# Attention and merge of a hybrid S5, attention and MoE layer: the work of GpSimd handed to VectorE and ScalarE, and VectorE operations joined in pairs

## The chip, the cores and the metric

The kernel runs on one core of one Trainium2 chip. The metric is the device time of one execution in microseconds (us); lower is better. All data are fp32. A matrix product is made from three products of split operands (high by high, high by low, low by high), so each operand exists as a high part and a low part.

## The reference, cut to what matters

One layer on 1024 latent tokens of width 1024, with 256 context tokens. The change touches the middle of it:

```python
p = softmax(concat([s_loc, s_ctx, sink], axis=-1))       # 8 heads; band of 3 blocks of 128 keys, 256 context keys
o = p_loc @ v_band + p_ctx @ v_ctx
z = gelu(y_ssm);  z = z * sigmoid(z @ w_glu + b_glu)
m = sigmoid(g_ssm) * (z @ w_ssm_out) + sigmoid(g_att) * (o @ w_att_out)
h = layer_norm(alpha * h + gate1 * (m @ w_o))
```

After it come the router, the mixture of experts (MoE, 32 experts, four for each token) and a last layer norm.

## The kernel before, in words

**Order of the work.** `pre` (line 143) holds everything ahead of the experts: input projections, the S5 scan, attention, GLU and merge; `moe` and `finish` follow. The stage of the change begins near 570 us and ends where the ranking of tokens by expert begins, near 1115 us. Attention (line 513) is the main stream there. `Filler.emit` (line 127) puts pieces of a second stream between its parts, 5.0 us of stated cost at a time (`FILL`), and the second stream is `tail` (line 217): `glu`, `ssm_out`, then `merge`. With every piece of `glu` and `ssm_out` goes one step of `residual` (line 708). Outside of `manual_schedule` blocks the framework's planner settles each engine's order when the kernel is built, from the written order and its own costs; inside such a block the engines that it names keep the written order. The end of `merge` (after `K.last`) keeps VectorE's written order. Each engine runs its instructions in the order that was settled, and all transfers of this stage are issued from one queue, SP.

**Attention.** Eight blocks of 128 queries, two groups of four heads. A call of `scores` (line 566) treats a pair of heads: matmuls to two `sa` tiles (128x384, local keys) and one `sb` tile (128x512, context keys of both heads) in PSUM; VectorE's maxima (lines 589, 590); then on 128x2 tiles the steps of lines 591 to 594 that give minus the maximum (`nm`) and the sink's exponent; ScalarE's exponentials into `P` with their sums (lines 598 to 603); VectorE's total and reciprocal (lines 604 to 606). At line 608 GpSimd (POOL) multiplies the two `P` tiles by it. There are 32 pairs, so 64 such products, 48 of 640 columns and 16 of 512. `values` (line 611) transposes `P` on TensorE, splits the transposes into `ph` (ScalarE) and `pl` (VectorE, line 43) and multiplies them with V.

**GLU.** `glu` (line 465) takes 256 tokens at a time, four times: per block `m` of 128 channels 12 matmuls into 256 columns of a PSUM bank of its own, a sigmoid on ScalarE (line 488), a product (line 489), a split into `K.zh` and `K.zl`. The PSUM pool `mm` has two banks.

**Merge.** `merge` (line 754) has four groups of 256 tokens; group g starts when attention has finished its two blocks of 128 queries. `branches` (line 806): 12 matmuls with `w_att_out` per block of 128 columns, a product with the gate (line 823), a sum (line 824), a split into `mh` and `ml` (line 825). `mix` (line 833), for groups 0 to 2: 24 matmuls per 128 tokens and 256 columns with `w_o`, a product (line 842) and a sum (line 843) into `h`. `norm` (line 850) makes layer norm and modulation, whose last sum (line 862) is POOL's. Group 3 goes through `mix_tile`, one tile of 128 tokens at a time.

**Weights of the merge.** `weights` (line 793) keeps up to two pieces of 1 MiB ready: it loads a piece raw and splits it, the high part on ScalarE, the low part in turn on POOL and VectorE (`eng=`, line 795). Over the four groups that are 22 pieces, eleven of them on POOL; two more pieces of `w_o` are split at line 242, so 24 in all. The same six pieces return for each group. Tiles `raw`, `whi` and `wlo` have two buffers each.

**Other work on POOL.** `residual` (lines 716, 721, 722) scales `xhat_d` by ALPHA and the gains, 16 pieces of 128x512 through memory and back; `consts` (lines 776 to 780); `residual2` (line 1552) makes two products of 128x512 for each tile of tokens, from memory for tiles 0 to 5 (`h is None`), from the tile on hand for 6 and 7.

Of the kernel before, what the change touches and what calls it, by code (L numbers as in the profile page):

```python
# [8 lines left out]
F32 = mybir.dt.float32  # L9
# [10 lines left out]
D = 1024  # L20
# [61 lines left out]
def body(tc, a, o):  # L82
# [3 lines left out]
    with es:  # L86
# [21 lines left out]
        K.cst = cst  # L108
        K.mask = cst.tile([128, 8, 2, 32], BF16, name="mask")
# [33 lines left out]
def pre(tc, a, K, top):  # L143
    nc = tc.nc
    es = ExitStack()
    with es:
# [88 lines left out]
        with ExitStack() as ws:  # L235
# [6 lines left out]
            K.wo = [load_w(tc, K, a["w_o"][:, c * 256:(c + 1) * 256], to=[wo.tile([128, KT, 256], F32R, name="wo%d%d" % (c, i)) for i in range(2)])  # L242
                    for c in range(2)]
# [221 lines left out]
def glu(tc, a, K, zp):  # L465
# [3 lines left out]
    for c in range(4):  # L469
# [13 lines left out]
        for m in range(4):  # L483
            p = K.mm.tile([128, 512], F32, tag="mm", name="mm")
            p = p[:, 0:256]
            mm3(nc, p, w, (zh, zl), 4, lambda x, k: x[:, k, m * 128:(m + 1) * 128], lambda x, k: x[:, k, :])
            g = zp.tile([128, 256], F32, tag="zsig", bufs=2, name="zsig")
            nc.scalar.activation(out=g, in_=p, func=ACTF.Sigmoid, bias=K.cols[:, 48 + m:49 + m])
            nc.vector.tensor_tensor(g, g, zt[:, m, :], ALU.mult)
            split(nc, K.zh[:, m, t0:t0 + 256], K.zl[:, m, t0:t0 + 256], g)  # L490
            if m % 2:
                yield 2.8
# [20 lines left out]
def attention(tc, a, K, es, fl):  # L513
# [16 lines left out]
    nc.sync.dma_start(out=sink, in_=a["sink"].unsqueeze(0).to_broadcast([128, 8]))  # L530
    KH = kp.tile([128, 2, S + NCTX], F32R, name="KH")
# [34 lines left out]
    def scores(n, kv, pr, Q):  # L566
# [25 lines left out]
        nc.vector.scalar_tensor_tensor(nm, nm, 0.125, sink[:, hs], ALU.mult, ALU.max)  # L592
        nc.vector.tensor_tensor(su[:, 2], sink[:, hs], nm, ALU.subtract)
        nc.vector.tensor_scalar(nm, nm, -1.0, None, ALU.mult)
# [9 lines left out]
        nc.vector.tensor_tensor(su[:, 0], su[:, 0], su[:, 1], ALU.add)  # L604
        nc.vector.tensor_tensor(su[:, 0], su[:, 0], su[:, 2], ALU.add)
        nc.vector.reciprocal(su[:, 0], su[:, 0])  # L606
        for i in range(2):
            nc.gpsimd.tensor_scalar(P[i][:, 0:nl + 256], P[i][:, 0:nl + 256], su[:, 0, i:i + 1], 1.0, ALU.mult, ALU.mult)  # L608
# [99 lines left out]
def residual(tc, a, K, es):  # L708
# [3 lines left out]
    for c in range(2):  # L712
# [3 lines left out]
        nc.gpsimd.tensor_scalar(gb, gb, ALPHA, 1.0, ALU.mult, ALU.mult)  # L716
        for t in range(8):
# [3 lines left out]
            nc.gpsimd.tensor_tensor(x, x, gb[:, 0], ALU.mult)  # L721
            nc.gpsimd.tensor_tensor(x, x, gb[:, 1], ALU.add)
# [30 lines left out]

def merge(tc, a, K, es):
# [16 lines left out]
    def consts():  # L771
# [4 lines left out]
        nc.gpsimd.tensor_tensor(x0, x0, G2, ALU.mult)  # L776
        nc.gpsimd.tensor_tensor(B2, B2, x0, ALU.add)
        x0 = hp.tile([128, D], F32, tag="xm", name="x0")
        nc.sync.dma_start(out=x0, in_=a["ln_rows"][0:1, :].to_broadcast([128, D]))
        nc.gpsimd.tensor_tensor(G2, G2, x0, ALU.mult)  # L780
# [7 lines left out]
    sources = [s for g in range(4) for s in  # L788
               [(a["w_att_out"][:, c * 512:(c + 1) * 512], 512, 4) for c in range(2)] +
               [(a["w_o"][:, c * 256:(c + 1) * 256], 256, 8) for c in range(0 if g < 3 else 2, 4)]]  # L790
    ready = []

    def weights():
        while len(ready) < 2 and sources:
            ready.append(load_w(tc, K, *sources.pop(0), eng=nc.gpsimd if len(sources) % 2 else None))
        return ready.pop(0)
# [9 lines left out]
    def branches(g, raw, gs, mh, ml):  # L806
# [5 lines left out]
        for c in range(4):  # L812
# [179 lines left out]
    for g in range(4):  # L992
# [25 lines left out]
        for t in late:  # L1018
            yield t
# [1225 lines left out]
```

## Time and profile before

| | |
|---|---|
| median of 3 runs | 2791.53 us (2789.71 to 2792.7) |
| the profiled execution | 2796.39 us, span 2794.6 us |
| busy over the span | TensorE (PE) 90%, VectorE (DVE) 80%, ScalarE (ACT) 52%, GpSimd (POOL) 17% |
| TensorE's granted clock, mean | 0.943 of 2.4 GHz |
| moved by DMA | 631.11 MB, mean 226 GB/s |

The span is cut into 40 slices on the profile's page, so the stage of the change is slices 9 to 16. A busy engine is not an engine at its peak. Idle time in a row is charged to what ended it. DMA share is the mean busy share of the 16 DMA engines.

### The profile page before, as it was taken

To read this page: it belongs to the slowest core of one execution; us is meant where nothing else is said; L and a number is where in the kernel's file an instruction comes from. 1 tells how busy PE (TensorE), PEld (TensorE's weight loads), DVE (VectorE), ACT (ScalarE), POOL (GpSimd) and SP (SyncE) were. 2 spreads that over 40 slices of the span, in tenths; PEclk is the share of its full clock that TensorE was granted. 3 is DMA by queue.
4 is the path that set the end of the run, shared out by engine and by line. 5 is a ranking of instruction groups with operands and counts; after the bars stand their busy time and mean duration, and the time that the engine had idled before them with its cause. 6 is when DMAs were issued, how large, how long until landed. Compare 5 with 4: busy or idle time off the path is not lost. (4 is left out here: it accounts for less than half of the span.)

```text
span 2794.6 us, 41588 instructions
## 1 busy us (share of the span) xinstructions
PE 2523.9 (90%) x14030; PEld 2123.3 (76%) x14030; DVE 2234.2 (80%) x4306; ACT 1465.9 (52%) x2352; POOL 465.0 (17%) x303
## 2 busy tenths in 40 slices
PE   6799999978887877699999999999999999999990
PEld 1698887767686767588888888889888887888770
DVE  9636796347788887788878888888988899899995
ACT  0623113656555422455656666666666666666661
POOL 3200000034333243210110110110111011101113
PEclk8799999979998877699999999999999999999995
DMA  7434623554454463678979978988998999899983
GB/s 252 155 125 157 202 87 116 161 172 136 163 169 139 146 195 102 209 244 266 290 226 284 295 242 283 292 273 272 303 294 262 305 301 300 275 305 302 311 280 144
DMA packets 409674, 631.11 MB, mean 226 GB/s; under 512 B 36497, under 2 KB 215569, under 8 KB 408497
## 3 DMA queue, kind: packets, MB, share of 16 engines
q1 hardware_dynamic: 397152, 584.37, 63.8%
q0 software_dynamic: 11872, 42.47, 6.5%
q8 instruction: 112, 1.84, 0.3%
q10 hardware_dynamic: 432, 1.57, 0.2%
q14 instruction: 106, 0.86, 0.1%
HBM read 551.76 MB, written 76.57 MB: 225 GB/s over the span
## 5 line engine op out<-in xcount | busy, mean ns | idle before, releaser
L1478 DVE TENSOR_TENSOR wl<-raw,wh 128x1024 fp32r<-128x1024 f32 x768 | 920.8, 1219 | 163.4 <-ACT wh L1476 162.3
L1476 ACT ACTIVATE wh<-raw 128x1024 fp32r<-128x1024 f32 x768 | 790.3, 1052 | 246.5 <-PE dn L1294 87.9
L1344 PE MATMUL uw<-x,wh 128*128 128x320 f32 (+5 forms) x1920 | 581.3, 366 | 0.2 <-issue 0.2
L1345 PE MATMUL uw<-x,wl 128*128 128x192 f32 (+4 forms) x1920 | 501.4, 261 | 0.0
L1344 PEld LDWEIGHTS uw<-x,wh 128*128 128x128 f32 x1920 | 364.3, 190 | 24.0 <-issue 0.3
L1345 PEld LDWEIGHTS uw<-x,wl 128*128 128x128 f32 x1920 | 369.6, 193 | 0.5
L1291 PE MATMUL dn<-wh,a 128*128 128x512 f32 (+4 forms) x752 | 298.7, 397 | 0.0
L1292 PE MATMUL dn<-wl,a 128*128 128x512 f32 (+4 forms) x752 | 293.6, 390 | 0.0
L1427 POOL DMA_INDIRECT acc_d<-y,wi x47 | 120.4, 2562 | 958.3 <-DVE y L1425 816.3
L1294 PE MATMUL dn<-wh,a 128*128 128x512 f32 (+3 forms) x608 | 238.5, 392 | 0.6 <-DVE a L1271 0.6
L1291 PE MATMUL up<-wh,x 128*128 128x512 f32 x544 | 221.8, 408 | 0.0
L1294 PE MATMUL up<-wh,x 128*128 128x512 f32 x544 | 213.0, 392 | 0.0
L1292 PE MATMUL up<-wl,x 128*128 128x512 f32 x544 | 212.3, 390 | 0.0
L1356 ACT ACTIVATE t<-uw,bias 128x160 f32<-128x160 f32 (+5 forms) x240 | 98.6, 419 | 134.5 <-PE uw L1345 131.6
L1291 PEld LDWEIGHTS dn<-wh,a 128*128 128x128 f32 (+4 forms) x752 | 135.7, 180 | 37.8 <-issue 4.1
L1292 PEld LDWEIGHTS dn<-wl,a 128*128 128x128 f32 (+4 forms) x752 | 135.8, 181 | 33.9
L608 POOL TENSOR_SCALAR P<-P,su 128x640 f32<-128x640 f32 (+1 forms) x64 | 55.1, 874 | 608.0 <-DVE su L606 543.9
L1294 PEld LDWEIGHTS dn<-wh,a 128*128 128x128 f32 (+3 forms) x608 | 112.8, 186 | 28.4 <-DVE a L1271 2.7
L42 ACT ACTIVATE whi<-raw 128x2048 fp32r<-128x2048 f32 x38 | 72.8, 1917 | 112.9 <-PE mm L53 72.5
L1240 POOL DMA_INDIRECT x<-xm_d,ri x47 | 53.3, 1135 | 463.3 <-DVE L L1202 304.0
L1291 PEld LDWEIGHTS up<-wh,x 128*128 128x128 f32 x544 | 102.3, 188 | 27.4 <-issue 8.4
L1294 PEld LDWEIGHTS up<-wh,x 128*128 128x128 f32 x544 | 102.1, 188 | 22.4
(532 smaller groups left out, 5349.2 us busy)
## 6 DMA issues: line engine op xcount, KB each, us to landing
raw<-w_gate_up SPq DMA_DIRECT2D x512, 512.0 KB
raw<-w_down SPq DMA_DIRECT2D x256, 512.0 KB
mw<-w_mod SPq DMA_DIRECT2D x64, 256.0 KB
raw<-w_o SPq DMA_DIRECT2D x16, 1024.0 KB
raw<-w_in SPq DMA_DIRECT2D x13, 1024.0 KB
raw<-w_mod SPq DMA_DIRECT2D x8, 1024.0 KB
gate_d<-gs SPq DMA_DIRECT2D x16, 512.0 KB
raw<-w_att_out SPq DMA_DIRECT2D x8, 1024.0 KB
```

Source lines behind the costliest of these rows:

```text
L42: nc.scalar.activation(out=hi, in_=src, func=ACTF.Copy)
L608: nc.gpsimd.tensor_scalar(P[i][:, 0:nl + 256], P[i][:, 0:nl + 256], su[:, 0, i:i + 1], 1.0, ALU.mult, ALU.mult)
L1240: nc.gpsimd.indirect_dma_start(out=x[0:nb], out_offset=None, in_=K.xm_d, bounds_check=S - 1, oob_is_err=True, in_offset=bass.IndirectOffse ...
L1291: nc.tensor.matmul(ps, lhsT=h, rhs=wh[:, k], start=st, stop=False)
L1292: nc.tensor.matmul(ps, lhsT=h, rhs=wl[:, k], start=False, stop=en and nb <= 64)
L1294: nc.tensor.matmul(ps, lhsT=X[:, k0 + k, lo:lo + nb], rhs=wh[:, k], start=False, stop=en)
L1344: nc.tensor.matmul(p[:, 0:2 * n], lhsT=wh[:, k, fs], rhs=self.x[:, k, 0:2 * n], start=k == 0, stop=False)
L1345: nc.tensor.matmul(p[:, 0:m], lhsT=wl[:, k, fs], rhs=self.x[:, k, 0:m], start=False, stop=k == KT - 1)
L1356: nc.scalar.activation(out=y[i], in_=self.uw[i][:, 1], func=ACTF.Identity, bias=self.bias[:, q * 8 + j0 + i:q * 8 + j0 + i + 1])
L1427: nc.gpsimd.indirect_dma_start(out=K.acc_d, out_offset=bass.IndirectOffsetOnAxis(ap=wi[0:nb], axis=0), in_=o[0:nb], in_offset=None, bounds ...
L1476: nc.scalar.activation(out=h, in_=r, func=ACTF.Copy)
L1478: nc.vector.tensor_tensor(l, r, h, ALU.subtract)
```

## The change: what it does

- GLU: two blocks of 128 channels share one PSUM bank, each with its own matmuls and sigmoid; product and split are made once on 512 columns.
- Softmax: the sign is taken into a constant (`nsink`), and the total is one `reduce_sum`; lines 591 to 594 and 604 to 606 become five operations. The products with `P` go to ScalarE.
- Residual, constants, the last sum of `norm`, and `residual2` for tiles 0 to 5 go from POOL to VectorE. Tiles 6 and 7 keep POOL.
- Weights: `parts` splits each of the six pieces once (ScalarE and VectorE), writes both parts to memory, and loads both parts (2 MiB) at every later use, 18 times.
- Merge: both blocks of a step share one PSUM bank; product, sum and split are made on 512 columns. `h` becomes one tile of 128x2x1024.

```diff
@@ -239,8 +241,7 @@
...
             residual2_consts(tc, a, K, pool(ws, "res2"))
-            K.wo = [load_w(tc, K, a["w_o"][:, c * 256:(c + 1) * 256], to=[wo.tile([128, KT, 256], F32R, name="wo%d%d" % (c, i)) for i in range(2)])
-                    for c in range(2)]
+            K.wo = [parts(tc, a, K, "o", c, [wo.tile([128, KT, 256], F32R, name="wo%d%d" % (c, i)) for i in range(2)]) for c in range(2)]
             while not K.last:
...
@@ -480,16 +481,17 @@
...
         yield 1.0
-        for m in range(4):
+        for m in (0, 2):
             p = K.mm.tile([128, 512], F32, tag="mm", name="mm")
-            p = p[:, 0:256]
-            mm3(nc, p, w, (zh, zl), 4, lambda x, k: x[:, k, m * 128:(m + 1) * 128], lambda x, k: x[:, k, :])
-            g = zp.tile([128, 256], F32, tag="zsig", bufs=2, name="zsig")
-            nc.scalar.activation(out=g, in_=p, func=ACTF.Sigmoid, bias=K.cols[:, 48 + m:49 + m])
-            nc.vector.tensor_tensor(g, g, zt[:, m, :], ALU.mult)
-            split(nc, K.zh[:, m, t0:t0 + 256], K.zl[:, m, t0:t0 + 256], g)
-            if m % 2:
-                yield 2.8
+            g = zp.tile([128, 2, 256], F32, tag="zsig", bufs=2, name="zsig")
+            for j in range(2):
+                n = m + j
+                pj = p[:, j * 256:(j + 1) * 256]
+                mm3(nc, pj, w, (zh, zl), 4, lambda x, k: x[:, k, n * 128:(n + 1) * 128], lambda x, k: x[:, k, :])
+                nc.scalar.activation(out=g[:, j], in_=pj, func=ACTF.Sigmoid, bias=K.cols[:, 48 + n:49 + n])
+            nc.vector.tensor_tensor(g, g, zt[:, m:m + 2, :], ALU.mult)
+            split(nc, K.zh[:, m:m + 2, t0:t0 + 256], K.zl[:, m:m + 2, t0:t0 + 256], g)
+            yield 2.8
 
...
@@ -528,6 +530,8 @@
...
     nc.sync.dma_start(out=sink, in_=a["sink"].unsqueeze(0).to_broadcast([128, 8]))
+    nsink = cp.tile([128, 8], F32, name="nsink")
+    nc.vector.tensor_scalar(nsink, sink, -1.0, None, ALU.mult)
     KH = kp.tile([128, 2, S + NCTX], F32R, name="KH")
...
@@ -589,9 +593,8 @@
...
         nc.vector.tensor_tensor(nm, mx[:, 0], mx[:, 1], ALU.max)
-        nc.vector.scalar_tensor_tensor(nm, nm, 0.125, sink[:, hs], ALU.mult, ALU.max)
-        nc.vector.tensor_tensor(su[:, 2], sink[:, hs], nm, ALU.subtract)
-        nc.vector.tensor_scalar(nm, nm, -1.0, None, ALU.mult)
+        nc.vector.scalar_tensor_tensor(nm, nm, -0.125, nsink[:, hs], ALU.mult, ALU.min)
+        nc.vector.tensor_tensor(su[:, 2], sink[:, hs], nm, ALU.add)
         P = []
...
@@ -601,11 +604,10 @@
...
         nc.scalar.activation(out=su[:, 2], in_=su[:, 2], func=ACTF.Exp)
-        nc.vector.tensor_tensor(su[:, 0], su[:, 0], su[:, 1], ALU.add)
-        nc.vector.tensor_tensor(su[:, 0], su[:, 0], su[:, 2], ALU.add)
-        nc.vector.reciprocal(su[:, 0], su[:, 0])
+        nc.vector.reduce_sum(nm, su.rearrange("p a i -> p i a"), axis=AX.X)
+        nc.vector.reciprocal(nm, nm)
         for i in range(2):
-            nc.gpsimd.tensor_scalar(P[i][:, 0:nl + 256], P[i][:, 0:nl + 256], su[:, 0, i:i + 1], 1.0, ALU.mult, ALU.mult)
+            nc.scalar.activation(out=P[i][:, 0:nl + 256], in_=P[i][:, 0:nl + 256], func=ACTF.Copy, scale=nm[:, i:i + 1])
         return P
...
@@ -713,13 +715,13 @@
...
         nc.sync.dma_start(out=gb, in_=a["ln_rows"][2:4, cs].unsqueeze(0).to_broadcast([128, 2, 512]))
-        nc.gpsimd.tensor_scalar(gb, gb, ALPHA, 1.0, ALU.mult, ALU.mult)
+        nc.vector.tensor_scalar(gb, gb, ALPHA, None, ALU.mult)
         for t in range(8):
...
             nc.sync.dma_start(out=x, in_=d)
-            nc.gpsimd.tensor_tensor(x, x, gb[:, 0], ALU.mult)
-            nc.gpsimd.tensor_tensor(x, x, gb[:, 1], ALU.add)
+            nc.vector.tensor_tensor(x, x, gb[:, 0], ALU.mult)
+            nc.vector.tensor_tensor(x, x, gb[:, 1], ALU.add)
             nc.sync.dma_start(out=d, in_=x)
...
@@ -751,6 +753,22 @@
...
 
+def parts(tc, a, K, m, c, to=None):
+
+    nc = tc.nc
+    kt, n = (4, 512) if m == "a" else (KT, 256)
+    hi, lo = to or (K.wp.tile([128, kt, n], F32R, tag=t, name=t) for t in ("whi", "wlo"))
+    if (m, c) in K.parts:
+        for t, d in zip((hi, lo), K.parts[m, c]):
+            nc.sync.dma_start(out=t.bitcast(F32), in_=d)
+    else:
+        load_w(tc, K, a["w_att_out" if m == "a" else "w_o"][:, c * n:(c + 1) * n], n, kt, to=(hi, lo))
+        K.parts[m, c] = [K.dram.tile([128, kt, n], F32, name="w%s%d%d" % (m, c, i)) for i in range(2)]
+        for t, d in zip((hi, lo), K.parts[m, c]):
+            nc.sync.dma_start(out=d, in_=t.bitcast(F32))
+    return hi, lo
+
+
 def merge(tc, a, K, es):
...
@@ -773,11 +791,11 @@
...
         nc.sync.dma_start(out=x0, in_=a["ln_rows"][1:2, :].to_broadcast([128, D]))
-        nc.gpsimd.tensor_tensor(x0, x0, G2, ALU.mult)
-        nc.gpsimd.tensor_tensor(B2, B2, x0, ALU.add)
+        v.tensor_tensor(x0, x0, G2, ALU.mult)
+        v.tensor_tensor(B2, B2, x0, ALU.add)
         x0 = hp.tile([128, D], F32, tag="xm", name="x0")
         nc.sync.dma_start(out=x0, in_=a["ln_rows"][0:1, :].to_broadcast([128, D]))
-        nc.gpsimd.tensor_tensor(G2, G2, x0, ALU.mult)
+        v.tensor_tensor(G2, G2, x0, ALU.mult)
         x0 = hp.tile([128, D], F32, tag="xm", name="x0")
...
@@ -785,14 +803,12 @@
...
 
-    sources = [s for g in range(4) for s in
-               [(a["w_att_out"][:, c * 512:(c + 1) * 512], 512, 4) for c in range(2)] +
-               [(a["w_o"][:, c * 256:(c + 1) * 256], 256, 8) for c in range(0 if g < 3 else 2, 4)]]
+    sources = [s for g in range(4) for s in [("a", c) for c in range(2)] + [("o", c) for c in range(0 if g < 3 else 2, 4)]]
     ready = []
...
         while len(ready) < 2 and sources:
-            ready.append(load_w(tc, K, *sources.pop(0), eng=nc.gpsimd if len(sources) % 2 else None))
+            ready.append(parts(tc, a, K, *sources.pop(0)))
         return ready.pop(0)
...
@@ -815,14 +831,13 @@
...
                 w = weights()
+            p = K.mm.tile([128, 512], F32, tag="mm", name="mm").rearrange("p (i n) -> p i n", i=2)
             for i in range(2):
                 n = c % 2 * 2 + i
-                p = K.mm.tile([128, 512], F32, tag="mm", name="mm")[:, 0:256]
-                mm3(nc, p, w, (oh, ol), 4, lambda x, k: x[:, k, n * 128:(n + 1) * 128], lambda x, k: x[:, k, :])
-                u = gt[:, i, :]
-                v.tensor_tensor(u, p, u, ALU.mult)
-                v.tensor_tensor(u, u, sm[:, i, :], ALU.add)
-                split(nc, mh[:, c * 2 + i, :], ml[:, c * 2 + i, :], u)
+                mm3(nc, p[:, i], w, (oh, ol), 4, lambda x, k: x[:, k, n * 128:(n + 1) * 128], lambda x, k: x[:, k, :])
+            v.tensor_tensor(gt, p, gt, ALU.mult)
+            v.tensor_tensor(gt, gt, sm, ALU.add)
+            split(nc, mh[:, c * 2:c * 2 + 2, :], ml[:, c * 2:c * 2 + 2, :], gt)
             yield 2.7
...
@@ -835,12 +850,11 @@
...
             rn = part(g, c + 1) if c < 3 else None
+            p = K.mm.tile([128, 512], F32, tag="mm", name="mm").rearrange("p (i n) -> p i n", i=2)
             for i in range(2):
-                p = K.mm.tile([128, 512], F32, tag="mm", name="mm")[:, 0:256]
-                mm3(nc, p, (mh, ml), w, KT, lambda x, k: x[:, k, i * 128:(i + 1) * 128], lambda x, k: x[:, k, :])
-                u = gp.tile([128, 256], F32, tag="u", bufs=1, name="u")
-                v.tensor_tensor(u, p, g1[:, cs], ALU.mult)
-                v.tensor_tensor(h[i][:, cs], u, r[:, i, :], ALU.add)
+                mm3(nc, p[:, i], (mh, ml), w, KT, lambda x, k: x[:, k, i * 128:(i + 1) * 128], lambda x, k: x[:, k, :])
+            v.tensor_tensor(h[:, :, cs], p, g1[:, cs].unsqueeze(1).to_broadcast([128, 2, 256]), ALU.mult)
+            v.tensor_tensor(h[:, :, cs], h[:, :, cs], r, ALU.add)
             r = rn
...
@@ -859,14 +873,14 @@
...
             v.tensor_tensor(x, h[i], G2, ALU.mult)
-            nc.gpsimd.tensor_tensor(x, x, B2, ALU.add)
+            v.tensor_tensor(x, x, B2, ALU.add)
             nc.sync.dma_start(out=K.xm_d[t * 128:(t + 1) * 128, :], in_=x)
...
         t = 6 + i
-        h = hp.tile([128, D], F32, tag="h", name="h")
+        h = h67[:, i]
         st = K.sm2.tile([128, 4, 6], F32, tag="l3st", name="l3st")
...
@@ -1013,8 +1027,9 @@
...
             break
-        h = [hp.tile([128, D], F32, tag="h", name="h") for _ in range(2)]
+        h = hp.tile([128, 2, D], F32, tag="h", bufs=1, name="h")
         yield from mix(g, r, mh, ml, h, late)
+        h = [h[:, i] for i in range(2)]
         for t in late:
...
@@ -1025,6 +1040,7 @@
...
 
+    h67 = hp.tile([128, 2, D], F32, tag="h", bufs=1, name="h")
     for h6, gates6, modulated6 in mix_tile(0, mh, ml, late):
...
@@ -1549,7 +1565,7 @@
...
             x = h[:, cs]
-        nc.gpsimd.tensor_tensor(x, x, K.ga[:, cs], ALU.mult)
+        (nc.gpsimd if h is not None else v).tensor_tensor(x, x, K.ga[:, cs], ALU.mult)
         xs.append(x)
...
     for c, x in enumerate(xs):
```

## Rows read from the trace of the kernel before

**Rows 1.** Windows: length; PE, PEld, DVE, ACT, POOL busy; PE clock, DMA share, GB/s.
```profile
570.00:665.00 95.00, 68.35 (x388) 58.68 (x388) 55.50 (x98) 57.49 (x114) 52.01 (x44) 0.80 0.47 158
665.00:750.00 85.00, 79.10 (x429) 63.13 (x428) 61.44 (x142) 48.15 (x122) 20.09 (x18) 1.00 0.43 145
750.00:955.00 205.00, 165.05 (x1138) 145.84 (x1136) 173.06 (x420) 106.59 (x269) 75.71 (x49) 0.90 0.47 152
955.00:1070.00 115.00, 82.78 (x491) 73.46 (x490) 89.47 (x164) 37.40 (x58) 45.77 (x23) 0.78 0.60 192
```

**Rows 2.** What TensorE waited for, 570 to 1070: total us, times, longest.
```profile
PE pv L633 <- DVE pl L43: 15.8, 7, 3.7
PE pv L632 <- DVE of L642: 11.9, 3, 7.0
PE tp L621 <- issue: 11.8, 1, 11.8
PE sa L583 <- ACT P L598: 10.7, 8, 3.9
PE mm L51 <- DVE gg L823: 10.3, 3, 5.6
PE tp L933 <- POOL xm L862: 8.0, 1, 8.0
...
PE mm L51 <- ACT zsig L488: 3.6, 3, 2.1
```

**Rows 3.** Timeline of VectorE: start us, duration us, instruction.
```profile
834.11 0.16 DVE L594 TENSOR_SCALAR nm<-nm 128x2 f32<-128x2 f32 x1
...
849.11 3.98 DVE L594 TENSOR_SCALAR nm<-nm 128x2 f32<-128x2 f32 x1
```

**Rows 4.** Timeline of GpSimd over the same time.
```profile
848.56 4.50 POOL L43 TENSOR_TENSOR wlo<-raw,whi 128x2048 fp32r<-128x2048 f32 x1
```

**Rows 5.** Windows 570 to 1070 by tile: su, nm, zsig, gg, u; DVE busy first.
```profile
570.00:1070.00 500.00, 35.16 (x124) 6.26 (x31) 53.78 (x62) 0.87 0.49 161
570.00:1070.00 500.00, 41.99 (x124) 65.65 (x248) 0.87 0.49 161
570.00:1070.00 500.00, 22.29 (x32) 13.79 (x32) 0.87 0.49 161
570.00:1070.00 500.00, 52.17 (x96) 12.70 (x32) 0.87 0.49 161
570.00:1070.00 500.00, 24.48 (x48) 0.87 0.49 161
```

**Rows 6.** Groups on VectorE, 570 to 1070: busy us, mean ns | idle before.
```profile
L43 DVE TENSOR_TENSOR wlo<-raw,whi 128x2048 fp32r<-128x2048 f32 x13 | 30.7, 2362 | 7.0 <-ACT whi L42 7.0
...
L593 DVE TENSOR_TENSOR su<-sink,nm 128x2 f32<-128x2 f32 x31 | 13.7, 442 | 0.8
...
L508 DVE TENSOR_TENSOR gs<-mm,gs 128x512 f32<-128x512 f32 x16 | 11.0, 688 | 3.4 <-PE mm L53 3.1
```

**Rows 7.** The page's costliest group (expert stage).
```profile
L1478 DVE TENSOR_TENSOR wl<-raw,wh 128x1024 fp32r<-128x1024 f32 x768 | 920.8, 1219 | 163.4 <-ACT wh L1476 162.3
```

**Rows 8.** Groups on GpSimd, 570 to 1130, with what ended its idle time.
```profile
L721 POOL TENSOR_TENSOR x<-x,gb 128x512 f32<-128x512 f32 x16 | 21.8, 1364 | 18.4 <-DMA x<-xhat_d 18.2
...
L1552 POOL TENSOR_TENSOR x<-x,ga 128x512 f32<-128x512 f32 x12 | 17.6, 1482 | 37.4 <-DMA x<-xhat_d 19.5 <-DVE pT L1116 15.3 <-DVE x L1561 2.6
```

**Rows 9.** Groups on ScalarE, 570 to 1070.
```profile
L42 ACT ACTIVATE whi<-raw 128x2048 fp32r<-128x2048 f32 x24 | 46.1, 1920 | 43.5 <-PE mm L53 23.3 <-PE mm L52 13.0 <-DVE h L843 7.2
...
L42 ACT ACTIVATE mh<-gg 128x256 fp32r<-128x256 f32 x32 | 12.7, 420 | 34.8 <-DVE gg L824 34.7
```

**Rows 10.** DMA from 570 to 1070, all queues.
```profile
DMA packets 58474, 80.54 MB, mean 161 GB/s; under 512 B 6792, under 2 KB 40712, under 8 KB 58248
```

**Rows 11.** SP's queue, a transfer of 1536 KB: start and duration of its issue.
```profile
745.75 0.47 SPq L772 DMA_DIRECT2D rb<-rows_d  x1
```

**Rows 12.** VectorE's first reader of that transfer.
```profile
755.71 0.69 DVE L773 TENSOR_SCALAR rb<-rb 128x1024 f32<-128x1024 f32 x1 [0.24 <-DMA rb<-rows_d]
```

More of the change, by code (lines that the diff above doesn't have):

```diff
@@ L108, in body @@
         K.cst = cst
+        K.dram = dram
+        K.parts = {}
         K.mask = cst.tile([128, 8, 2, 32], BF16, name="mask")
@@ L950, in choose @@
         su = K.sm2.tile([128, 1], F32, tag="tsu", name="tsu")
-        oh = gp.tile([128, 256], F32, tag="u", bufs=1, name="oh")[:, 0:128].rearrange("p (k e) -> p k e", k=4)
+        oh = gp.tile([128, 128], F32, tag="u", bufs=1, name="oh").rearrange("p (k e) -> p k e", k=4)
         over = oh.rearrange("p k e -> p e k")
```

## The prediction

> **What bounds the kernel now.** I read the windows of the stage first, then what TensorE waits for, then the timelines of VectorE and GpSimd at the worst gap, last the groups of each engine. In the 500 us from 570 to 1070 TensorE is busy for 68.35 + 79.10 + 165.05 + 82.78 = 395.3 us and idle for 104.7 us [rows 1]. Only the second stretch is close to TensorE's own rate (79.1 of 85 us, clock 1.00). In the others the clock is 0.80, 0.90 and 0.78, a mixture of 2.4 and 1.2 GHz; as time at the lower level that is 0.4 x 95 + 0.2 x 205 + 0.44 x 115 = 130 us, and it lies where TensorE has its gaps. So the stage is not bound by one engine's total; it is a chain that passes through TensorE, VectorE and ScalarE, and the names behind TensorE's gaps are mostly VectorE's [rows 2].
>
> Why VectorE is late is in the timelines. An operation on 128x2 elements takes 0.16 us at 834.11 and 3.98 us at 849.11 [rows 3]; the second began while GpSimd split a weight piece, a job of 4.50 us that began at 848.56, and ended as that ended [rows 4]. The same shows in sums. The seven small softmax operations cost 35.16 + 41.99 - 13.7 = 63.5 us for 31 pairs (line 593 stands in both tile rows) [rows 5, 6], 2.05 us a pair where seven bare ones would be 1.12. So GpSimd's 52.0 + 20.1 + 75.7 + 45.8 = 193.6 us [rows 1] cost little by themselves, but hold VectorE up.
>
> **The change part by part.** VectorE first, with a bare 512-wide product at 0.69 us [rows 6] and a 1024-wide one at 1.22 us [rows 7].
> - Softmax: 32 pairs x 2.05 = 65.6 us become 32 x 5 x 0.16 = 25.6 (the new sum over six columns is priced as a small operation; ends 0.16 and 0.69 would make it 17 us more at worst). Saves 40.
> - GLU: 22.3 us [rows 5] become 16 x 0.69 = 11.0. Saves 11.
> - Branches: 52.2 us [rows 5] become 16 x 3 x 0.69 = 33.1. Saves 19.
> - Mix: 24.5 us [rows 5] become 12 x 2 x 0.69 = 16.6. Saves 8.
> - Weights: thirteen of the splits at 2.36 us [rows 6] become six. Saves 16.5.
> - Moved in from GpSimd: 32 + 12 operations of 512 columns (residual, residual2) at 0.69 and 11 of 1024 (constants, norm) at 1.22. Adds 30.4 + 13.4 = 44.
> Net about -51 us of VectorE's 379 in the stage [rows 1], with no GpSimd to wait for.
>
> ScalarE gets 64 scalings of P. From 0.42 us for 256 columns and 1.92 for 2048 [rows 9] a column is 0.84 ns, so 0.74 us for 640 and 0.63 for 512: 48 x 0.74 + 16 x 0.63 = 46 us. GpSimd's own time, 53.8 us [rows 5], is the upper end, if the scale from a tile costs more. It loses 18 weight splits, 18 x 1.92 = 35 us, and some 5 us by wider copies. Net +6 us on 250 [rows 1]: hidden, since ScalarE is half idle; were it not, the whole 46 would stand behind the reciprocal of each pair.
>
> DMA: 24 loads of 1 MiB become 6 loads, 12 stores and 36 loads, 30 MiB or 31.5 MB more. The shares of rows 1 make 247 us of all 16 engines for 80.54 MB [rows 10], 326 GB/s; so the addition is 97 us, and the sum 344 us fits into a stage of some 450. SP issues 30 transfers more, 30 x 0.47 = 14 us [rows 11], and in its queue a load that waits for a weight buffer stands before those for gates, sums and queries. A load of parts can start only when the matmuls of the piece before the last have freed its buffer; it then has the time of one piece to land. A load of 1.5 MiB was issued at 745.75 and its reader ran at 755.71, 10 us later [rows 11, 12], so 2 MiB takes up to 13 us, and 6.4 us at the full rate. By the code a group uses six pieces; the third stretch covers a little over two groups, so some thirteen pieces in 205 us, 16 us each, and eight in the 115 us of the fourth, 14 us each. I take this at nothing; the cover is attention's work between two pieces, thin in the fourth stretch.
>
> GLU puts two blocks into one bank, with the sigmoid of the first between their matmuls. No row shows TensorE at a bank that ScalarE is reading. The nearest is TensorE's wait for the sigmoid to free a bank, 2.1 us at the longest [rows 2]: between 0 and 8 x 2.1 = 17 us. I take 4, as attention's matmuls can stand between. The Trainium skill, PSUM — Partial Sum Buffer, section on bank collisions, says that two engines may not touch one bank in the same partitions at a time and that software must keep them apart; by it the second half would always wait, and the sum would come out 13 us higher, near 2758.
>
> VectorE also takes over waits for transfers: GpSimd stood 18.2 us before line 721 and 19.5 us before line 1552 until data came [rows 8]. On GpSimd nothing queued behind; on VectorE the softmax does, and TensorE behind that. Ends 0 and 37.7 us; I take 2, the low side, since the planner orders VectorE by when data should be there. The products of line 1552 for the last two tiles stand in VectorE's written order, on the path: 4 x 0.69 = 3 us.
>
> **What it gives back.** Of TensorE's waits [rows 2] those that GpSimd makes go: 11.9 (line 642), 10.3 (823) and 8.0 (its own sum at 862). Half of the 11.8 goes (the first transposes, behind softmax steps held up in the same way), and a third of 15.8 (pl) and of 10.7 (exponentials, behind line 594); the rest of these is their normal chain, and becomes the next late thing. That is 11.9 + 10.3 + 8.0 + 5.9 + 5.3 + 3.6 = 45 us. With fewer gaps the clock is up for longer. The 130 us at the lower level cost at most half of TensorE's work in them, 0.5 x 0.79 x 130 = 51 us; I take a fifth, 10 us, since the gaps shrink rather than vanish. 45 + 10 - 4 - 2 - 3 = 46 us. The profiled execution took 2796.4 us (span 2794.6 and 1.8 around it), so 2750.4 by its time; it lies 4.9 us above the median of the runs, 2791.5, so the forecast is **2745 us**. The expert stage behind is untouched and moves forward as a whole.
>
> **Rivals.**
> - TensorE becomes the bound: all waits of rows 2 but the sigmoid's go (68.5 us) and half of the clock's cost (25 us), 2698 us. For it: VectorE falls to 328 us. Against: the chains of softmax and GLU stay serial.
> - The shared bank always holds TensorE: 17 us in place of 4, 2758 us. For it: the sigmoid stands between the matmuls in the written order. Against: there are other matmuls to run.
> - VectorE stands behind transfers: 37.7 us in place of 2, 2781 us. For it: rows 8, and more traffic. Against: the residual has a whole group's time.
> - **Slower: reloaded weights come late.** If pieces follow each other at their own matmuls' pace, 48 matmuls at 85 / 429 = 0.20 us [rows 1] are 9.5 us against 13.3 us of landing: 3.8 us each, 18 x 3.8 = 68 us against 46 gained, 2813 us. It decides from 12 late pieces on (46 / 3.8). For it: the depth of prefetch falls from raw and split pairs to split pairs alone, and the share is 0.60 in the last stretch. Against: 16 us between pieces while attention runs, which holds for most of them.
> - It moves nothing: the planned order hands the freed time to other waits, 2791 us.
>
> **How the numbers follow.** Chances: forecast 0.50, TensorE as the bound 0.13, bank 0.12, VectorE behind transfers 0.09, late weights 0.10, nothing 0.06. What a measurement of this kernel can tell from no change is about 0.2%, 5.6 us. Faster: 0.50 + 0.13 + 0.12 + 0.09 = 0.84; within it 0.06; slower 0.10. The range from 2700 to 2785 holds the forecast with its bounds, both milder rivals and nearly all of the first; outside are late weights and no change, and a little of the best case.
>
> **What would show it.** Right: GpSimd all but empty from 570 to 1060; small softmax operations at 0.16 us each, none above 1 us; VectorE near 330 us in the stage; TensorE's waits for lines 642, 823 and 862 gone; the clock above 0.9 in the first and third stretch; ranking of the last tile some 46 us earlier. Wrong: TensorE waiting for a DMA into whi or wlo (late weights); VectorE idle until xhat_d has come; TensorE waiting for the sigmoid in eight places; or shorter gaps and the same end. Should the end of attention come earlier by 40 us but the ranking by less, the fourth stretch has turned into one of transfers.

## The result, and the profile after

| | before | after |
|---|---|---|
| median of 4 runs of each, on one chip | 2790.62 us | 2748.19 us |
| lowest and highest | 2785.92 to 2792.7 | 2745.94 to 2751.04 |
| the profiled execution, its span | 2796.39, 2794.6 us | 2747.31, 2745.2 us |
| TensorE's granted clock, mean | 0.943 | 0.948 |
| moved by DMA | 631.11 MB | 662.55 MB |

The ratio is 0.9851, 95% interval 0.9834 to 0.9868: 42 us faster. The forecast was 2745 us; the sum was right, and the experiments show that several of its terms were not. The two profiled executions lie 49.1 us apart, mostly because the one before is 5.8 us above the median here; times read from the traces carry that.

The windows of the stage after the change; columns as in [rows 1]:

```profile
570.00:665.00 95.00, 74.55 (x431) 64.67 (x431) 58.59 (x115) 66.06 (x130) 0.00 (x0) 0.86 0.43 149
665.00:750.00 85.00, 80.73 (x456) 64.31 (x456) 62.22 (x136) 58.59 (x142) 0.00 (x0) 1.00 0.65 226
750.00:955.00 205.00, 182.72 (x1301) 163.10 (x1299) 162.97 (x393) 118.28 (x294) 7.20 (x7) 0.95 0.78 276
955.00:1070.00 115.00, 91.60 (x528) 78.25 (x527) 72.44 (x197) 18.70 (x47) 14.98 (x15) 0.77 0.60 219
```

GpSimd is empty for the first 180 us and busy for 22 of the other 320. In the third stretch TensorE does 1301 instructions where it did 1138 [rows 1]. The last stretch holds later work than before, so from here on I go by landmarks. The scalings of P end at 919.8 us, before at 956.4; the last output of attention (the second addition into `of`) at 931.4, before at 976.9; the router's last pick (the last MAX8) at 1067.9, before at 1116.7. The 45.5 us between the two ends of attention are nearly the whole gain; the last pick adds 3.3, and the expert stage behind it moves as a whole (its first down projection at 1159.0 for 1208.3).

From 570 us to the last pick, before and then after (columns as above):

```profile
570.00:1116.70 546.70, 436.57 (x2700) 377.28 (x2699) 414.54 (x929) 260.70 (x592) 211.08 (x149) 0.87 0.47 153
570.00:1067.90 497.90, 429.01 (x2707) 369.93 (x2706) 354.36 (x827) 260.09 (x607) 22.12 (x21) 0.90 0.65 231
```

For the same work TensorE is idle for 110.1 us before and 68.9 after, and busy for 7.6 us less: 41 us are waits, some 8 us go with the clock (0.90 for 0.87).

What TensorE waited for from 570 to 1070 us (total us, times, longest):

```profile
PE pb L1574 <- DVE x L1577: 10.2, 3, 4.2
PE tp L623 <- ACT zt L481: 8.5, 3, 6.2
PE pv L635 <- DVE pl L43: 7.7, 7, 2.6
PE sa L587 <- ACT P L601: 6.9, 6, 2.6
...
PE mm L53 <- DMA wlo<-wa: 3.2, 1, 3.2
...
PE pv L634 <- DVE of L644: 2.2, 2, 1.6
...
PE mm L51 <- DVE gg L838: 0.2, 1, 0.2
```

Against [rows 2]: the wait for `of` fell from 11.9 to 2.2 us, for the branches from 10.3 to 0.2, for `pl` from 15.8 to 7.7, and the 8.0 us for GpSimd's sum are gone. New is a wait for a transfer of a weight part (3.2 us, and 0.4 for another `wlo`); the wait before residual2's matmuls grew from 1.9 us, up to the last pick before, to 10.2.

Groups on VectorE and ScalarE in the same 500 us (busy us, mean ns | idle before):

```profile
L838 DVE TENSOR_TENSOR gg<-mm,gg 128x512 f32<-128x512 f32 x16 | 10.9, 685 | 14.0 <-PE mm L53 13.5 <-DMA gg<-gate_d 0.4
...
L597 DVE TENSOR_TENSOR su<-sink,nm 128x2 f32<-128x2 f32 x31 | 5.7, 185 | 0.6
L608 DVE RECIPROCAL nm<-nm 128x2 f32<-128x2 f32 x31 | 5.0, 161 | 0.5
...
L607 DVE TENSOR_REDUCE nm<-su 128x2 f32<-128x6 f32 x31 | 4.8, 156 | 12.7 <-ACT su L606 12.2 <-ACT P L603 0.4
L610 ACT ACTIVATE P<-P,nm 128x640 f32<-128x640 f32 x48 | 37.2, 822 | 8.8 <-DVE nm L608 8.1 <-DVE l1t L70 0.5
```

The subtraction from `sink` takes 185 ns where it took 442 [rows 6]; the new sum over six columns costs what a small operation costs.

### The profile page after: what moved, and what is told of

The parts are those of the page before. It is cut to its first block, busy times and chain, and to the rows that moved or that the text cites. A ratio compares the mean times of both kernels' runs of the same rounds, so it can differ in the third digit from the quotient of the medians.

```text
span 2745.2 us, 41252 instructions
## 1 busy us (share of the span) xinstructions
PE 2513.9 (92%) x14030; PEld 2115.1 (77%) x14030; DVE 2175.9 (79%) x4203; ACT 1465.1 (53%) x2368; POOL 275.4 (10%) x173
## 2 busy tenths in 40 slices
DMA packets 400934, 662.55 MB, mean 241 GB/s; under 512 B 36976, under 2 KB 203760, under 8 KB 393616
## 4 chain that ended last, share of the span: by engine, by line
PE 46%; DVE 6%; issue 4%; DMA 2%; ACT 1%; POOL 0%; POOLq 0%; SPq 0%; DVEq 0%; ACTq 0%
PE uw L1360 14%; PE uw L1361 7%; PE dn L1307 6%; PE dn L1308 6%; PE dn L1310 5%; DVE wl L1494 2%; PE tp L1278 2%; PE up L1307 2%; PE up L1310 2%; PE up L1308 2%; DMA acc_d<-y,wi 1%; DVE oh L1198 1%; PE sl L1214 1%; ACT wh L1492 1%; PE up L1321 1%
## 5 line engine op out<-in xcount | busy, mean ns | idle before, releaser
L1308 PEld LDWEIGHTS up<-wl,x 128*128 128x128 f32 x544 | 102.4, 188 | 18.8
L51 PE MATMUL mm<-whi,uh 128*128 128x256 f32 x320 | 108.2, 338 | 4.7 <-DVE r L307 4.7
L52 PE MATMUL mm<-wlo,uh 128*128 128x256 f32 x320 | 107.5, 336 | 0.0
```

The costliest lines, as they stand in the source:

```text
L51: nc.tensor.matmul(out, lhsT=lsel(lh, k), rhs=rsel(rh, k), start=start and k == 0, stop=False)
L52: nc.tensor.matmul(out, lhsT=lsel(lh, k), rhs=rsel(rl, k), start=False, stop=False)
L1308: nc.tensor.matmul(ps, lhsT=h, rhs=wl[:, k], start=False, stop=en and nb <= 64)
```

## The experiments

The question was which part earns the 42 us: GpSimd's absence, fewer and longer VectorE operations, or the weight parts kept in DRAM. Column "held" is worked out from each trace: of every VectorE operation between 560 and 1100 us the time above the median of its shape in e3_splits, added up where it is more than 0.15 us (for 48 splits of 256 columns in before, e1_no_pool and e12_short, a shape that e3_splits lacks, the median is their own kernel's). "Wide" is the joined VectorE operations, "parts" the weight parts kept in DRAM. "Ratio" is to the kernel before on the same chip. Several chips were used, on which the kernel before has medians of 2789.1 to 2791.9 us, so a difference of two medians is uncertain by some 3 us from that alone.

| kernel | P scaled on | GpSimd's other jobs | wide | parts | median us | ratio, 95% interval | held us |
|---|---|---|---|---|---|---|---|
| before | GpSimd | there | no | no | 2790.6 | | 74.9 |
| after | ScalarE | gone | yes | yes | 2748.2 | 0.9851 [0.9834, 0.9868] | 11.2 |
| e1_no_pool | ScalarE | gone | no | no | 2745.8 | 0.9832 [0.9814, 0.9849] | 12.5 |
| e2_wide_only | GpSimd | there | yes | no | 2784.5 | 0.9979 [0.9967, 0.9991] | 75.6 |
| e3_splits | ScalarE | gone | yes | no | 2742.5 | 0.9830 [0.9812, 0.9848] | 10.9 |
| e4_p_pool | GpSimd | gone | yes | yes | 2743.2 | 0.9834 [0.9817, 0.9850] | 14.7 |
| e5_rest_pool | ScalarE | there | yes | no | 2773.6 | 0.9957 [0.9942, 0.9972] | 71.4 |
| e6_splits_pool | ScalarE | splits only | yes | no | 2774.8 | 0.9946 [0.9933, 0.9960] | 39.8 |
| e7_res_pool | ScalarE | residual only | yes | no | 2750.4 | 0.9862 [0.9833, 0.9891] | 27.3 |
| e8_p_pool_splits | GpSimd | gone | yes | no | 2734.8 | 0.9806 [0.9777, 0.9835] | 16.0 |
| e9_idle_tt | ScalarE | idle work | yes | no | 2767.1 | 0.9911 [0.9895, 0.9928] | 41.5 |
| e10_idle_ts | ScalarE | idle work | yes | no | 2763.3 | 0.9896 [0.9879, 0.9912] | 32.0 |
| e11_half_parts | GpSimd | gone | yes | group 1 | 2738.0 | 0.9806 [0.9790, 0.9822] | 15.7 |
| e12_short | GpSimd | gone | no | no | 2753.4 | 0.9872 [0.9856, 0.9889] | 16.9 |

### GpSimd or the number of operations

e1_no_pool, on the kernel before (all of GpSimd's jobs of the stage in the same manner):

```diff
-            nc.gpsimd.tensor_scalar(P[i][:, 0:nl + 256], P[i][:, 0:nl + 256], su[:, 0, i:i + 1], 1.0, ALU.mult, ALU.mult)
+            nc.scalar.activation(out=P[i][:, 0:nl + 256], in_=P[i][:, 0:nl + 256], func=ACTF.Copy, scale=su[:, 0, i:i + 1])
...
-            ready.append(load_w(tc, K, *sources.pop(0), eng=nc.gpsimd if len(sources) % 2 else None))
+            ready.append(load_w(tc, K, *sources.pop(0)))
...
-            nc.gpsimd.tensor_tensor(x, x, gb[:, 0], ALU.mult)
+            nc.vector.tensor_tensor(x, x, gb[:, 0], ALU.mult)
```

> The kernel before, with GpSimd's work of the stage (scaling of P, every second weight split, residual, constants, norm) moved to ScalarE and VectorE and nothing else: seven small softmax operations, 256-column GLU, branches and mix stay. Theory 'held up' (VectorE's short operations wait for GpSimd's, and this is what costs the time): small operations fall to 0.16 us although VectorE's bare work rises (44 us moved in, 12 splits x 2.36 = 28 us), and the kernel is 20 to 45 us faster than before, 2745 to 2770. Theory 'count' (the gain is from fewer and longer VectorE operations): VectorE has more to do and not less, so no gain or a loss, 2790 to 2830.

e2_wide_only is its opposite: the changed kernel with these lines as they were, and no parts.

> The changed kernel with all of GpSimd's work put back where it was (scaling of P, every second weight split without parts in DRAM, residual, constants, norm); five small operations a pair and 512 columns stay. 'Held up': the small operations are again 1 to 4 us where GpSimd runs, and the gain over before is 0 to 15 us, 2775 to 2791. 'Count': most of the gain stays, 2745 to 2760.

Measured: 2745.8 and 2784.5 us. Taking work from GpSimd alone brings the whole gain; widening alone 0.2%. The window of the third stretch in e1_no_pool, and two small operations:

```profile
750.00:955.00 205.00, 174.80 (x1242) 154.97 (x1242) 179.15 (x447) 135.51 (x302) 2.32 (x2) 0.94 0.51 168
```

```profile
L594 DVE TENSOR_SCALAR nm<-nm 128x2 f32<-128x2 f32 x31 | 5.0, 161 | 0.3
L593 DVE TENSOR_TENSOR su<-sink,nm 128x2 f32<-128x2 f32 x31 | 4.8, 153 | 0.3
```

VectorE is busier than before here (179.15 us for 173.06 [rows 1]; 400.6 for 379.5 over all four stretches), and the kernel is 46 us faster: not VectorE's load but its standing still was the price. From 570 us to the last pick TensorE is idle for 72.8 us in e1_no_pool and for 108.5 in e2_wide_only, against 110.1 before. In e2_wide_only three of the five small operations are slow again (468, 280 and 240 ns in the mean; the sum and the reciprocal stay at 153 and 161). The slowest:

```profile
L595 DVE TENSOR_TENSOR nm<-mx 128x2 f32<-128x2 f32 x31 | 14.5, 468 | 1.3
```

### Which of GpSimd's jobs

e4_p_pool puts only the scaling of P back:

```diff
-            nc.scalar.activation(out=P[i][:, 0:nl + 256], in_=P[i][:, 0:nl + 256], func=ACTF.Copy, scale=nm[:, i:i + 1])
+            nc.gpsimd.tensor_scalar(P[i][:, 0:nl + 256], P[i][:, 0:nl + 256], nm[:, i:i + 1], 1.0, ALU.mult, ALU.mult)
```

> The changed kernel with one thing put back: P is scaled by GpSimd (64 operations, 53.8 us) and not by ScalarE (51 us). 'Held up': the reduce_sum and reciprocal of one pair stand behind the scaling of another, small operations rise above 0.3 us in the mean, and the time is 10 to 35 us above the changed kernel, 2758 to 2783. 'Count': nothing on VectorE's list has changed and ScalarE is relieved, so the same time or a few us less, 2740 to 2750.

Measured: 2743.2 us, so the scaling does no harm on GpSimd. Its groups on GpSimd, then the same small operation on VectorE:

```profile
L610 POOL TENSOR_SCALAR P<-P,nm 128x640 f32<-128x640 f32 x48 | 44.7, 944 | 185.8 <-DVE nm L608 80.0 <-ACT ph L42 45.9 <-PE sa L590 26.4
```

```profile
L595 DVE TENSOR_TENSOR nm<-mx 128x2 f32<-128x2 f32 x31 | 4.8, 156 | 0.8
```

156 ns beside some 55 us of GpSimd's work: its jobs are short (803 ns in the median of the 64) and start when VectorE has just finished this pair's reciprocal. Only 4.6 us of "held" fall on them. So 'held up', as I had put it for this run, fell; either the other jobs do it, or the scaling of P stood behind them in GpSimd's queue. Three runs for that; e5_rest_pool is e2_wide_only with P on ScalarE; e6_splits_pool is e3_splits (the changed kernel without parts, below) with every second split's subtraction on GpSimd:

```diff
-            ready.append(parts(tc, a, K, *sources.pop(0)))
+            ready.append(parts(tc, a, K, *sources.pop(0), eng=nc.gpsimd if len(sources) % 2 else None))
```

and e7_res_pool is e3_splits with the residual (its two constants in the same way):

```diff
-            nc.vector.tensor_tensor(x, x, gb[:, 0], ALU.mult)
-            nc.vector.tensor_tensor(x, x, gb[:, 1], ALU.add)
+            nc.gpsimd.tensor_tensor(x, x, gb[:, 0], ALU.mult)
+            nc.gpsimd.tensor_tensor(x, x, gb[:, 1], ALU.add)
```

> As e2_wide_only, but P is scaled by ScalarE: GpSimd keeps every second weight split, residual, constants and norm, and nothing of the softmax waits in GpSimd's queue any more. 'Held up' (VectorE stands while GpSimd runs its two-operand operations): small operations stay above 0.25 us in the mean, and the time stays near e2_wide_only, 2770 to 2785. 'Queue' (the scaling of P stood behind residual and splits on GpSimd, 41 us in all in e2_wide_only between the reciprocal and the first scaling of a pair, against 10 us in e3_splits): the time falls to 2740 to 2755. Between them, by the 31 us of queue alone: 2753.

> As e3_splits, but every second weight split's second half (some 11 operations of 4.6 us) is on GpSimd again; residual and the rest stay on VectorE. 'Held up': VectorE is relieved of 11 x 2.36 = 26 us but stands behind 51 us of GpSimd's work; 5 to 20 us slower than e3_splits, 2748 to 2762. 'Queue': nothing else waits on GpSimd, so no loss and perhaps a gain by the relief, 2735 to 2745.

> As e3_splits, but the 32 products and sums of the residual and their two constants (45 us) are on GpSimd again, all else on VectorE and ScalarE. 'Held up': 5 to 20 us slower than e3_splits, 2748 to 2762. 'Queue': 2735 to 2745, as no other work is on GpSimd.

Measured: 2773.6, 2774.8 and 2750.4 us. Freeing the scaling of P from the queue gives 11 of the 42 us that separate e2_wide_only from e3_splits (2784.5 - 2742.5), or 6 by the ratios, whose intervals overlap; the rest stays: mainly 'held up'. Eleven weight splits alone cost 32 us, more than I had expected, although VectorE is relieved of eleven of its own; the residual's 32 short jobs cost 8, with intervals that overlap. VectorE and then GpSimd in e6_splits_pool:

```profile
894.70 0.68 DVE L850 TENSOR_TENSOR h<-h,r 128x512 f32<-128x512 f32 x1
895.29 4.50 DVE L595 TENSOR_TENSOR nm<-mx 128x2 f32<-128x2 f32 x1
899.70 0.08 DVE L961 MATCH_VALUE_LOAD tix<-tmx,lgs 128x8 f32 x1
```

```profile
895.06 4.70 POOL L43 TENSOR_TENSOR wlo<-raw,whi 128x2048 fp32r<-128x2048 f32 x1 [17.63 <-ACT whi L42]
```

Or did TensorE merely get its weights later, as GpSimd needs 4.7 us for a split? In e6_splits_pool it waits only 0.2 us for a `wlo` of GpSimd, but 9.9 us for two `whi` of ScalarE (2.0 us in e3_splits), so the trace leaves it open. e9_idle_tt leaves the split on VectorE and gives GpSimd the same work for nothing; e10_idle_ts does it in the form of P's scaling. In e9_idle_tt, for every second piece:

```diff
+    raw = load_raw(tc, K, src, n, kt)
+    load_w(tc, K, src, n, kt, to=(hi, lo), raw=raw)
+    if idle:
+        nc.gpsimd.tensor_tensor(raw, raw, hi.bitcast(F32), ALU.subtract)
```

and in e10_idle_ts in its place:

```diff
+        for _ in range(2):
+            nc.gpsimd.tensor_scalar(raw, raw, 1.0, 1.0, ALU.add, ALU.mult)
```

> As e3_splits (all splits by ScalarE and VectorE), and after every second split GpSimd does the same subtraction once more, from the raw piece and its high part back onto the raw piece, 11 times some 4.6 us, whose result nobody reads; only the next load into that buffer waits for it. 'Held up' (VectorE stands while GpSimd runs a long two-operand operation): 15 to 40 us slower than e3_splits, 2757 to 2785, with VectorE operations of 3 to 5 us beside it. 'Late' (in e6_splits_pool the splits came late because GpSimd takes 4.6 us where VectorE takes 2.36, and TensorE waited for the weights): nobody waits for this work, so 2740 to 2747.

> As e9_idle_tt, but the idle work on GpSimd has one operand from a tile and two constants, the form in which P is scaled, twice per piece for some 5.5 us in all. If only the two-operand form holds VectorE up: 2740 to 2748. If any long work of GpSimd does: near e9_idle_tt, 2757 or more.

Measured: 2767.1 and 2763.3 us, 25 and 21 above e3_splits. Work that nobody reads costs most of what the splits cost, and 'late' falls. So does the idea that only the two-operand form does it. VectorE around one of these jobs in e9_idle_tt, and the job:

```profile
920.59 0.15 DVE L607 TENSOR_REDUCE nm<-su 128x2 f32<-128x6 f32 x1
920.66 0.16 DVE L972 COPY mask<-mask 128x32 bf16<-128x32 bf16 x1
920.74 0.15 DVE L975 RECIPROCAL tsu<-tsu 128x1 f32<-128x1 f32 x1
920.81 0.14 DVE L608 RECIPROCAL nm<-nm 128x2 f32<-128x2 f32 x1
920.87 4.46 DVE L70 TENSOR_TENSOR l1t<-l1y 128x2 f32<-128x2 f32 x1
925.25 0.22 DVE L976 TENSOR_SCALAR tge<-tge,tsu 128x4 f32<-128x4 f32 x1
```

```profile
920.75 4.56 POOL L765 TENSOR_TENSOR raw<-raw,whi 128x2048 f32<-128x2048 f32 x1 [21.05 <-DVE nm L607]
```

The reciprocal at 920.81 passes while GpSimd works; the product of two tiles in SBUF behind it stands until 925.3, when the job ends, and with it everything queued on VectorE. Beside another of these jobs two products with a matmul's result and a maximum pass at their usual length, and the sum of two SBUF tiles (0.69 us by itself) stands until the job is over:

```profile
758.13 1.29 DVE L835 TENSOR_TENSOR gg<-mm,gg 128x512 f32<-128x512 f32 x2
...
760.18 0.56 DVE L593 TENSOR_REDUCE mx<-sa 128x1 f32<-128x384 f32 x1
760.65 1.41 DVE L836 TENSOR_TENSOR gg<-gg,gs 128x512 f32<-128x512 f32 x1
```

```profile
756.92 4.59 POOL L765 TENSOR_TENSOR raw<-raw,whi 128x2048 f32<-128x2048 f32 x1 [4.20 <-DVE wlo L43]
```

The planned order is not quite that of e3_splits from the first of these jobs on, and the next load into the raw buffer starts later; what of the 25 us is due to that I did not separate. "Held" rose by 31 us. Against e3_splits, the six wide runs that have more on GpSimd than the scaling of P (e2_wide_only, e5_rest_pool, e6_splits_pool, e7_res_pool, e9_idle_tt, e10_idle_ts) lose 0.5 to 1.1 us for each us of "held" that they have more.

### The parts, and a better version

e3_splits takes the weight parts out of the changed kernel:

```diff
-    if (m, c) in K.parts:
...
     load_w(tc, K, a["w_att_out" if m == "a" else "w_o"][:, c * n:(c + 1) * n], n, kt, to=(hi, lo))
-    K.parts[m, c] = [K.dram.tile([128, kt, n], F32, name="w%s%d%d" % (m, c, i)) for i in range(2)]
...
```

> The changed kernel without the parts in DRAM: every weight piece is loaded once as 1 MiB and split by ScalarE and VectorE (18 more splits of 1.92 us on ScalarE and 18 of 2.36 us on VectorE, 31.5 MB less DMA). 'Relief' (the parts take work off two engines that the chain needs): 15 to 40 us slower than the changed kernel, 2763 to 2790. 'Transfers' (the parts pay in the attention stretch what they cost after it, where the DMA engines are full): the end of attention some 10 us later, the time from there to the ranking some 10 us shorter, and the same time within 8 us, 2740 to 2756.

Measured: 2742.5 us, so 'relief' falls. From the end of attention to the last pick, after:

```profile
931.40:1067.90 136.50, 111.39 (x654) 95.93 (x653) 86.03 (x232) 22.72 (x59) 20.09 (x19) 0.77 0.67 247
```

and in e3_splits:

```profile
937.80:1064.90 127.10, 98.76 (x625) 86.19 (x623) 101.78 (x236) 35.93 (x66) 21.90 (x20) 0.82 0.53 169
```

The parts bring the end of attention 6.4 us forward and lose 9.4 us behind it, 3.0 us in these two traces together. Part of both is work that changed sides: behind the end of attention TensorE has 654 instructions for 625. It is not idle for longer there (25.1 us for 28.3), but busy for 12.6 us more, at a granted clock of 0.77 for 0.82. What else differs is SP's queue after the change (start us, duration us):

```profile
931.39 0.36 SPq L645 DMA_DIRECT2D o_d<-of  x1
...
940.74 3.20 SPq L763 DMA_DIRECT2D wo<-wo  x4
944.03 0.51 SPq L763 DMA_DIRECT2D whi<-wo  x1
944.59 0.50 SPq L763 DMA_DIRECT2D wlo<-wo  x1
...
945.68 0.87 SPq L763 DMA_DIRECT2D whi<-wo  x1
946.60 0.43 SPq L763 DMA_DIRECT2D wlo<-wo  x1
...
967.38 0.32 SPq L763 DMA_DIRECT2D whi<-wa  x1
...
971.86 0.94 SPq L1013 DMA_DIRECT2D oraw<-o_d  x2
```

Eight loads of 1 MiB are issued within 6.3 us, and the DMA engines are full:

```profile
930.00:940.00 10.00, 9.41 (x64) 8.95 (x65) 7.21 (x31) 2.13 (x6) 0.00 (x0) 0.83 1.03 382
...
950.00:960.00 10.00, 8.26 (x29) 5.90 (x29) 6.10 (x24) 2.19 (x8) 0.00 (x0) 0.50 1.02 420
```

The last group's attention output is read back 40 us after its last piece was stored; in e3_splits:

```profile
937.79 0.37 SPq L645 DMA_DIRECT2D o_d<-of  x1
...
961.67 0.42 SPq L1006 DMA_DIRECT2D oraw<-o_d  x1
```

24 us there. In between, after the change, the queue stands 9.7 us until TensorE has freed a weight buffer for the load at 967.38, the case that the prediction named and took at nothing:

```profile
SPq L763 <- PE mm L53: 9.7, 1, 9.7
```

No run changed the order of the loads alone, so that the queue is the reason is argued and not shown.

Then e3_splits and e4_p_pool in one, and, in e11_half_parts, parts for the one group that lies beside attention:

```diff
-    if (m, c) in K.parts:
+    if g == 1 and (m, c) in K.parts:
...
+        if g:
+            return hi, lo
         K.parts[m, c] = [K.dram.tile([128, kt, n], F32, name="w%s%d%d" % (m, c, i)) for i in range(2)]
```

> e3_splits and e4_p_pool in one: no parts in DRAM, and P scaled by GpSimd, which has nothing else to do in the attention stretch. If their two differences to the changed kernel (-5.7 and -5.0 us) are both real and add up, 2737; 'same' (they are differences in the planned order rather than gains): 2740 to 2748.

> As e8_p_pool_splits, but group 0 stores its split pieces and group 1, which falls into the attention stretch, loads them; groups 2 and 3 load raw pieces and split them. If the parts are worth 6 us to the end of attention there (931.4 against 937.8 us, changed kernel against e3_splits) and cost their 9 us only behind it: 2727 to 2733. If they are worth nothing while P is on GpSimd: 2734 to 2740.

Measured: 2734.8 and 2738.0 us, with the same ratio, 0.9806. That is what the two differences give if they add up, and e8_p_pool_splits is the fastest of all: 2% under the kernel before; its interval [0.9777, 0.9835] and the change's [0.9834, 0.9868] meet at their ends. Half the parts bring nothing. Last, the shortest edit, e1_no_pool with P left on GpSimd:

> The kernel before with only the long jobs taken from GpSimd: weight splits, residual, constants, norm and line 1552 go to VectorE; the scaling of P stays on GpSimd, the seven small softmax operations, 256-column GLU, branches and mix stay, and there are no parts in DRAM. If the whole gain lies in GpSimd's long jobs holding VectorE up, and widening, the move of P to ScalarE and the parts are worth nothing or less: 2734 to 2743, at least as fast as the changed kernel. If the wide operations or ScalarE's scaling are needed for it: 2750 to 2775.

Measured: 2753.4 us, the second of the two outcomes. Against the kernel before on its chip (2789.75 us) moving the long jobs alone gains 36 us. With P on GpSimd the wide operations are worth 19 us (2753.4 against 2734.8), with P on ScalarE 3 (2745.8 against 2742.5), in the kernel before 6 (2790.6 against 2784.5). In the same way ScalarE's scaling of P costs 5 and 8 us in the wide kernels and gains 8 in the narrow one. Every edit makes the planner write another order, and effects that turn with the other edits are of its size: single differences under some 8 us are not explained here.

## Why the prediction was right, point by point

- **A chain, bound by VectorE held up by GpSimd's work**: right, and shown by e1_no_pool and e9_idle_tt. 64 of 75 us of "held" are gone. The Trainium skill, GPSIMD Engine Reference, section Key points, says that GpSimd shares its SBUF interfaces with VectorE and contends with VectorE's instructions that have two SBUF inputs or run in a 2-port mode. The traces agree: products of two SBUF tiles stood up to 4.5 us, and matmul results with a tile from SBUF passed (`gg<-mm,gg`, two in 1.29 us beside a job of 4.59), as did reductions and reciprocals. Operations on one SBUF tile stood too (3.98 us [rows 3]; `tge<-tge,tsu` 4.54 us in e9_idle_tt); whether in a 2-port mode no trace shows.
- **The durations on VectorE**: right. Small operations 25.3 us (forecast 25.6), GLU 10.7 (11.0), branches 32.6 (33.1), mix 8.3 + 9.1 = 17.4 (16.6). "Near 330 us in the stage" was wrong, 356.2, since the 500 us now hold work that came later before; up to the last pick VectorE's time fell by 60 us (414.5 to 354.4), more than the 51 forecast. The sum of the forecast does not use this, rightly: e2_wide_only has the fewer operations and gains 6.
- **ScalarE, 46 us for the scaling**: 37.2 + 9.3 = 46.5 for the 62 of them in the window. "Hidden" is neither shown nor refuted: 5 to 8 us dearer than on GpSimd in two pairs (wide, without GpSimd's other jobs), cheaper in two (e1_no_pool against e12_short, e5_rest_pool against e2_wide_only).
- **The reload, "I take this at nothing"**: probably mis-sized. The 31.4 MB came as forecast, but the pace of 14 us a piece in the fourth stretch did not hold: eight loads were queued at a time. As a sum the parts cost 5.7 us (after against e3_splits) or 8.4 (e4_p_pool against e8_p_pool_splits). The intervals of each pair overlap, so the sign rests on two pairs together. The rival of late weights had the right place, at a small part of its price (3.6 us of TensorE's waits for `wlo`, not 68).
- **GLU's shared bank, 4 us**: no wait for the sigmoid is among TensorE's after the change; 3.6 before [rows 2]. By the rule of the Trainium skill, PSUM — Partial Sum Buffer, section on bank collisions, the second half has to stand behind the first sigmoid; the trace names no such wait of TensorE, and the 2758 us that it gave did not come.
- **VectorE's waits for transfers, 2 us**: 5.7 us before the residual's products and 4.0 before its constants for the same data; above the value taken, far from the 37.7.
- **Line 1552 for the last two tiles on VectorE, 3 us**: misread. The edit leaves them on GpSimd where the tile is at hand, and the trace after has four there, 1.37 us each.
- **The waits returned, 45 us**: 9.7 of 11.9 (`of`), 10.1 of 10.3 (`gg`), all of 8.0, 8.1 of 15.8 where 5.3 was forecast, 3.8 of 10.7 where 3.6 was, and 5.6 of 11.8 where 5.9 was. TensorE's idle time as a whole fell by 41.2 us, where 45 - 9 = 36 was forecast. The 9 us taken off (bank 4, transfers 2, line 1552 3) did not come under these names; the waits for `x` and `wlo` grew by some 12 instead (8.3 and 3.6). That the two are close is luck.
- **The clock, 10 us, and above 0.9 in the first and third stretch**: TensorE's busy time up to the last pick fell by 7.6 us; the granted clock is 0.95 in the third stretch, 0.86 in the first. There TensorE's gap of 11.8 us [rows 2] shrank to 6.2, the longest wait for `zt`, and did not go.
- **46 us earlier at the last pick**: 48.8 in the profiled pair, 42.4 by the medians. That attention alone would gain and the fourth stretch lose did not show in the sum (45.5 and 48.8); e3_splits takes 9.4 us less behind attention, part of it by work that lies before its end there.

## What to carry to other kernels

Before making an engine's operations fewer, see whether they are slow or merely stand: one shape with two durations (0.16 and 3.98 us [rows 3]) beside another engine's job is the sign, and moving such jobs paid 46 us (e1_no_pool) where fewer operations paid 6 (e2_wide_only). Work that did no harm on GpSimd beside a busy VectorE was in pieces of under a microsecond, placed where VectorE had just finished its own step (e4_p_pool). Data reloaded to spare engines may be paid for in the stretch where the transfers are dense; look at the DMA share there and at what stands behind the loads in the issuing queue, not at the mean.

## What was not expected of the hardware

- The prediction read from one pair of rows that a VectorE operation stands until the end of GpSimd's whole instruction. The runs add that it does so whether that has two operands (4.56 us, held 4.46) or one: in e10_idle_ts `su<-sink,nm` took 1.85 us beside the first of two jobs that took 3.91 together. GpSimd's total does not set the price: 11 jobs of 4.8 us cost 32 us, 32 jobs of some 1.5 us cost 8, 64 of some 0.8 us cost nothing that shows, each 48 to 56 us in all. But 22 jobs of 2.0 us, two in a row, cost 21 and 11 of 4.6 us whose result nobody reads 25, so the length of one job does not set it alone either; where a job meets VectorE was not varied by itself.
- GpSimd needed 4.6 us for a 128x2048 subtraction that VectorE does in 2.29, and VectorE stood 33.7 us for eleven of them in e6_splits_pool, 3.1 us each: handing such a job over cost VectorE more than doing it.
